# Two attention heads side by side in TensorE's array

## The chip, the cores and the metric

The kernel runs on one core of a Trainium2 chip. The metric is the device time of one execution in microseconds, the median of several runs. One execution was also traced by the hardware profiler; times inside the trace count from the start of its span.

## The reference, cut to what matters

Three transformer-like blocks work on 256 tokens with 1024 features in float32. Three parts of them are attention over heads of width 64, and one is a table lookup with the same shape of product:

```python
# block 1: causal attention, 16 heads (256 tokens are one block of keys)
s = einsum('bhqd,bhjd->bhqj', q, k); p = softmax(where(causal, s, -1e30)); o = einsum('bhqj,bhjd->bhqd', p, v)
# stick-breaking, 8 heads
z = einsum("bhtd,bhsd->bhts", q, k) * scale
a = where(before, exp(log_sigmoid(z) + after), 0.0); o = einsum("bhts,bhsd->bhtd", a, v)
# NSA, 8 heads in 2 groups: compressed, selected and window branches, weighted by gates
o = g[0] * o_c + g[1] * o_s + g[2] * o_w
# PEER routing: 8 heads, two halves of the query against two tables of 128 keys of width 64
```

## The kernel before, in words

Nearly all the work is products of 256 tokens with weights that are streamed from memory in blocks of 128 x 1024. `Stream` loads a block on SP's queue and splits it into two parts, `hi` on ScalarE (L247) and `lo` on VectorE (L248), and each product is three matmuls (`mm3`, L330 to L332; L395 to L397 where tokens lie on the partitions). A block is 24 such matmuls. These are called *ordinary* below.

The attention parts are generators. Each `yield` says what a step costs, and `pump` (L310) runs steps after each block of ordinary matmuls until the block's credit is used up. The framework then arranges the emitted instructions once more, by its own estimate of times, before the program is fixed; each engine runs its own list in that order and waits by semaphores.

A head has 64 features, so its score product uses only 64 of the 128 rows of TensorE's array, and its value product only 64 of the 128 columns. `tile_position` says which half. Two heads lie on the two halves of the partitions. A float32 matmul leaves two records in the trace.

- Block 1's attention, `moba`: `heads()` runs head by head: `scores(h)` (L673) with the softmax behind it on VectorE and ScalarE (`softmax_neg`, L744 to L751), and the three `transposes` (L680) of the head three before. `pv(u)` (L690, L692) makes the values of four heads.
- `stick_breaking`: `part1` (scores, L945 and L946), `part2` (sums by triangular matrices, L961 and L962), `part3` (values, L973 and L974), each two heads behind the one before.
- `nsa`: 16 units (head, branch): `scores` (L1080, L1081), `transposes` (L1087), `pv` (L1099, L1100, and for the second branch the compressed one, L1103). Its bias table `alibi` (L1072) is loaded on POOL's queue, and the pools of its tiles `sm_t`, `ptn` and `alibi` have two buffers each. It takes turns with the HGRN part.
- `routing`: 32 products per half of the tokens (L1408), first all of one row half `a`, then all of the other.

Of the kernel before, what the change touches and what calls it, by code (L numbers as in the profile page):

```python
# [21 lines left out]
P = 128  # L22
T = 256
# [82 lines left out]
def _vectors(inp):  # L106
    """Vectors over features, each as columns of 128."""
# [26 lines left out]
def _constants():  # L134
    """Tables that depend on the shapes alone, side by side in one array of 128 rows."""
# [72 lines left out]
# ---------------------------------------------------------------- the kernel  # L208
class Stream:
    """The weights, block by block: loaded ahead, each split exactly into two float32r parts."""  # L210

    def __init__(self, nc, w, names, raw, hl, ahead=2):
# [4 lines left out]
        # a second pool of two, for the blocks before the given one  # L217
# [10 lines left out]
    def _parts(self, b):  # L228
        # the first block in parts, so that the products start sooner
# [30 lines left out]
class K:  # L260
# [10 lines left out]
    # -- small helpers  # L271
# [23 lines left out]
    # Work that follows the products: `queue` in order, then `fill` (generators that yield what a step costs),  # L295
    # a little after each block of weights, so that the engines that feed the products are never blocked long.
# [30 lines left out]
    # -- products  # L327
# [6 lines left out]
    def lin(self, name, nm, nk, xh, xl, kpb=1, hooks=None, need=None, credit=1.45):  # L334
        """nm column tiles of 128, all of them for each row tile; out [features, tokens]."""
# [13 lines left out]
        # the last two blocks bank by bank, so that the first banks are done sooner  # L349
# [20 lines left out]
    def lin_tok(self, name, xh, xl, w=512, nch=2, hooks=None, credit=1.45):  # L370
        """tokens on partitions: acc[tt][ch] = [128 tokens, 512 features]"""
# [10 lines left out]
        # the last two blocks bank by bank  # L382
# [69 lines left out]
    def root(self, r, ss, width):  # L452
# [8 lines left out]
        # one Newton step: r *= 1.5 - 0.5 * (mean + eps) * r * r  # L461
# [5 lines left out]
    def spread(self, out, r):  # L467
        """The columns of r, by tokens, over the partitions: ones times a diagonal matrix."""
# [11 lines left out]
    # -- parts  # L480
# [139 lines left out]
    def moba(self, need):  # L620
# [3 lines left out]
        with ExitStack() as c:  # L624
# [5 lines left out]
            # two heads (each its first and its second half) on the partitions, pairs of heads in turn  # L630
# [925 lines left out]
```

## Time and profile before

| | |
|---|---|
| median of 3 runs | 1768.69 us (1767.66 to 1768.77) |
| span of the traced execution | 1763.3 us; no time beside the span is recorded for it |
| busy | TensorE 1747.2, VectorE 1311.7, ScalarE 895.1, POOL 27.5 us |
| mean granted TensorE clock | 0.999 |

PE is TensorE's matmuls, PEld its weight loads, DVE is VectorE, ACT ScalarE, SP the queue of the weight loads. In a row of a timeline, "x4" means that four consecutive records of the same line stand together; the second number is the time that they cover, the ends of matmuls being modelled.

### The profile page before, as it was taken

How to read it: one execution, taken by the hardware profiler on the slowest of the kernel's cores; microseconds unless marked ns; L12 is line 12 of the kernel's file. 1: busy time of each engine (PE TensorE's matmuls, PEld its weight loads, DVE VectorE, ACT ScalarE, POOL GpSimd, SP SyncE). 2: the span in 40 equal slices, each digit the busy share in tenths (PEclk: the TensorE clock that was granted, in tenths of full speed). 3: DMA queues.
4: the chain of work that ended last, by engine and by line, in shares of the span. 5: the costliest groups of instructions: out<-in, count | busy, mean ns of one | idle time of the engine just before them, and what ended most of it. 6: DMA issues, size and time to landing. Idle time of an engine off the chain costs nothing.

```text
span 1763.3 us, 33139 instructions
## 1 busy us (share of the span) xinstructions
PE 1747.2 (99%) x13299; PEld 1632.6 (93%) x13299; DVE 1311.7 (74%) x2532; ACT 895.1 (51%) x1324; POOL 27.5 (2%) x66
## 2 busy tenths in 40 slices
PE   8999999999999999999999999999999999999998
PEld 8999999879999998998799999999999888888886
DVE  7779966857997676766588989867776888855555
ACT  6466645556665647535456554533334443345443
POOL 0000000000000000100000000000000000000001
PEclk9999999999999999999999999999999999999999
DMA  7555565545556554632255464644445554455553
GB/s 243 186 180 182 181 200 189 176 135 169 182 178 199 183 176 138 209 114 84 63 192 192 156 206 152 205 133 156 152 148 167 165 171 155 156 179 191 191 191 119
DMA packets 87226, 297.25 MB, mean 169 GB/s; under 512 B 10784, under 2 KB 15680, under 8 KB 87072
## 3 DMA queue, kind: packets, MB, share of 16 engines
q1 hardware_dynamic: 84000, 288.92, 50.4%
q0 software_dynamic: 2640, 5.66, 1.3%
q8 instruction: 104, 1.70, 0.4%
q10 hardware_dynamic: 432, 0.56, 0.1%
q14 instruction: 50, 0.41, 0.1%
HBM read 292.03 MB, written 1.05 MB: 166 GB/s over the span
## 4 chain that ended last, share of the span: by engine, by line
PE 98%; ACT 1%; DVE 0%; issue 0%; DMA 0%; DVEq 0%
PE bank L330 22%; PE bank L331 21%; PE bank L332 21%; PE bank L1318 20%; PE bank L1529 4%; PE bank L396 1%; PE bank L395 1%; PE bank L397 1%; PE bank L673 1%; PE bank L1198 1%; PE bank L1099 1%; PE bank L1081 0%; PE bank L1408 0%; PE bank L1087 0%; PE bank L680 0%; PE bank L1080 0%
## 5 line engine op out<-in xcount | busy, mean ns | idle before, releaser
L247 ACT ACTIVATE hi<-raw 128x1024 fp32r<-128x1024 f32 (+2 forms) x552 | 574.0, 1046 | 731.3 <-PE bank L331 414.8
L248 DVE TENSOR_TENSOR lo<-raw,hi 128x1024 fp32r<-128x1024 f32 (+2 forms) x552 | 662.3, 1206 | 320.4 <-ACT hi L247 317.8
L330 PE MATMUL bank<-xh,hi 128*128 128x256 f32 x2624 | 748.2, 285 | 4.5 <-ACT hi L247 4.5
L331 PE MATMUL bank<-xl,hi 128*128 128x256 f32 x2624 | 743.6, 284 | 0.0
L332 PE MATMUL bank<-xh,lo 128*128 128x256 f32 x2624 | 742.4, 283 | 0.0
L330 PEld LDWEIGHTS bank<-xh,hi 128*128 128x128 f32 x2624 | 503.2, 192 | 9.0 <-ACT hi L247 4.7
L331 PEld LDWEIGHTS bank<-xl,hi 128*128 128x128 f32 x2624 | 503.0, 192 | 1.4 <-issue 1.2
L332 PEld LDWEIGHTS bank<-xh,lo 128*128 128x128 f32 x2624 | 502.7, 192 | 1.1 <-issue 1.1
L1318 PE MATMUL bank<-hi,xh 128*128 128x512 f32 x512 | 161.7, 395 | 0.0
L1318 PE MATMUL bank<-lo,xh 128*128 128x512 f32 x512 | 159.0, 390 | 0.0
L1318 PE MATMUL bank<-hi,xl 128*128 128x512 f32 x512 | 158.9, 390 | 0.0
L1318 PEld LDWEIGHTS bank<-lo,xh 128*128 128x128 f32 x512 | 96.1, 188 | 20.7 <-DVE lo L248 0.3
L1318 PEld LDWEIGHTS bank<-hi,xl 128*128 128x128 f32 x512 | 96.1, 188 | 20.1
L1318 PEld LDWEIGHTS bank<-hi,xh 128*128 128x128 f32 x512 | 94.2, 189 | 17.6
L332 PE MATMUL bank<-ah,lo 128*128 128x256 f32 x352 | 98.9, 281 | 0.0
L330 PE MATMUL bank<-ah,hi 128*128 128x256 f32 x352 | 98.6, 280 | 0.0
L331 PE MATMUL bank<-al,hi 128*128 128x256 f32 x352 | 97.9, 278 | 0.0
L1532 DVE SCALAR_TENSOR_TENSOR H<-bank,H 128x512 f32<-128x512 f32 x64 | 44.0, 687 | 43.4 <-PE bank L1529 43.4
L1529 PE MATMUL bank<-gi,oj 128*128 128x64 f16 x1024 | 74.3, 241 | 0.0
L1529 PEld LDWEIGHTS <-oj 128*128 128x128 f16 x1024 | 62.8, 118 | 9.8 <-issue 4.2
L330 PEld LDWEIGHTS bank<-ah,hi 128*128 128x128 f32 x352 | 66.2, 188 | 0.0
L331 PEld LDWEIGHTS bank<-al,hi 128*128 128x128 f32 x352 | 66.2, 188 | 0.0
(397 smaller groups left out, 1879.4 us busy)
## 6 DMA issues: line engine op xcount, KB each, us to landing
raw<-in_w_dram SPq DMA_DIRECT2D x540, 512.0 KB, 3.4
x<-in_x_dram SPq DMA_DIRECT2D x8, 128.0 KB, 4.1
raw<-in_w_dram SPq DMA_DIRECT2D x8, 128.0 KB, 4.2
alibi<-in_con_dram POOLq DMA_DIRECT2D x8, 128.0 KB, 2.4
raw<-in_w_dram SPq DMA_DIRECT2D x4, 256.0 KB, 4.1
q<-t SPq DMA_DIRECT2D x32, 32.0 KB, 3.2
k<-t SPq DMA_DIRECT2D x32, 32.0 KB, 1.9
wc<-in_wc_dram POOLq DMA_DIRECT2D x2, 512.0 KB, 5.7
```

The costliest lines, as they stand in the source:

```text
L247: nc.scalar.activation(hi[:, c], raw[:, c], AF.Copy)
L248: nc.vector.tensor_tensor(lo[:, c], raw[:, c], hi[:, c].bitcast(F32), ALU.subtract)
L330: mm(out, wh, xh, start=start, stop=False, skip_group_check=True)
L331: mm(out, wh, xl, start=False, stop=False, skip_group_check=True)
L332: mm(out, wl, xh, start=False, stop=stop, skip_group_check=True)
L395: mm(o, xh(k)[:, ts], hi[:, c], start=k == 0, stop=False, skip_group_check=True)
L396: mm(o, xl(k)[:, ts], hi[:, c], start=False, stop=False, skip_group_check=True)
L397: mm(o, xh(k)[:, ts], lo[:, c], start=False, stop=k == NK - 1, skip_group_check=True)
L673: nc.tensor.matmul(o, qa[:, qs], ka[:, 0:ke], start=qs.start == 0, stop=True, skip_group_check=True, tile_position=(rs.start, 0))
L1318: nc.tensor.matmul(acc[tt][n], x[:, s, tt * P:(tt + 1) * P], w[u][:, n * 512:(n + 1) * 512], start=i == 0 and x is self.xh and u == 0, sto ...
L1529: nc.tensor.matmul(b[:, t], oj[:, t // 4, :, t % 4], gi[:, n, t // 4, :, t % 4], start=t + n == 0, stop=n == 1, skip_group_check=True)
L1532: nc.vector.scalar_tensor_tensor(H[:, :, pt], pb.rearrange("p t i -> p i t"), 1.0 / GSCALE, H[:, :, pt], ALU.mult, ALU.mult)
```

## The change: pairs of heads

Two heads that lie on different halves go through all steps together. Their score matmuls alternate between the row halves and fill a bank each; their value matmuls alternate between the column halves. `scores(u)` now takes a pair and returns two banks, the softmax is called by the loop, and the loops of the generators are written anew, with more steps of smaller cost. In block 1 the transposes follow one pair behind instead of three heads. The diff, cut to its core (the values in `stick_breaking` and `nsa` are changed in the way of `moba`'s, and its scores in the way of `moba`'s):

```diff
-            def scores(h):
-                b = self.bank()
-                rs = slice(64 * (h % 2), 64 * (h % 2) + 64)
-                qa, ka = q[rs, h // 2], k[rs, h // 2]
-                for o, qs, ke in ((b[:, 0:128], slice(0, 128), 128), (b[:, 128:384], slice(128, 256), 256)):
-                    nc.tensor.matmul(o, qa[:, qs], ka[:, 0:ke], start=qs.start == 0, stop=True, skip_group_check=True,
-                                     tile_position=(rs.start, 0))
-                return self.softmax_neg(p2, b, causal[:, 128:], causal)
+            def scores(u):
+                bs = [self.bank() for _ in range(2)]
+                for o, qs, ke in ((slice(0, 128), slice(0, 128), 128), (slice(128, 384), slice(128, 256), 256)):
+                    for i in range(2):
+                        rs = slice(64 * i, 64 * i + 64)
+                        nc.tensor.matmul(bs[i][:, o], q[rs, u, qs], k[rs, u, 0:ke], start=qs.start == 0, stop=True,
+                                         skip_group_check=True, tile_position=(64 * i, 0))
+                return bs
...
             def pv(u):
                 b = self.bank()
-                for h in range(4 * u, 4 * u + 4):
-                    o = 256 * (h // 2 % 2)
-                    oo = b[64 * (h % 2):64 * (h % 2) + 64, o:o + 256]
-                    hs = slice(64 * h, 64 * h + 64)
-                    nc.tensor.matmul(oo, v[:, 0, hs], pt[:, h, 0:256], start=h % 4 < 2, stop=False, skip_group_check=True,
-                                     tile_position=(0, 64 * (h % 2)))
-                    nc.tensor.matmul(oo[:, 128:], v[:, 1, hs], pt[:, h, 256:384], start=False, stop=True, skip_group_check=True,
-                                     tile_position=(0, 64 * (h % 2)))
+                for h0 in (4 * u, 4 * u + 2):
+                    o = 256 * (h0 // 2 % 2)
+                    for kt in range(2):
+                        for i in range(2):
+                            h = h0 + i
+                            oo = b[64 * i:64 * i + 64, o + 128 * kt:o + 256]
+                            nc.tensor.matmul(oo, v[:, kt, 64 * h:64 * h + 64], pt[:, h, 0:256] if kt == 0 else pt[:, h, 256:384],
+                                             start=kt == 0 and h % 4 < 2, stop=kt == 1, skip_group_check=True, tile_position=(0, 64 * i))
...
-                for h in range(H + 3):
+                for h in range(0, H + 2, 2):
                     if h < H:
                         self.need(("rope", h // 8))
-                        pr[h] = scores(h)
-                    if h >= 3:
-                        transposes(h - 3, pr.pop(h - 3))
-                    yield 0.7
-                    while "v" in st and 4 * n + 3 <= h - 3:
+                        bs = scores(h // 2)
+                    for i in range(2):
+                        if h >= 2:
+                            transposes(h - 2 + i, pr.pop(h - 2 + i))
+                        if h < H:
+                            pr[h + i] = self.softmax_neg(p2, bs[i], causal[:, 128:], causal)
+                        yield 0.7
+                    while "v" in st and 4 * n + 3 < h:
...
-            for h in range(12):
-                if h < 8:
-                    s1[h] = part1(h)
-                if 0 <= h - 2 < 8:
-                    s2[h - 2] = part2(h - 2, *s1.pop(h - 2))
-                if 0 <= h - 4 < 8:
-                    part3(h - 4, s2.pop(h - 4))
-                yield 0.9
+            for u in range(6):
+                if u >= 2:
+                    part3(u - 2, s2.pop(u - 2))
+                if 0 <= u - 1 < 4:
+                    s2[u - 1] = []
+                    for s in s1.pop(u - 1):
+                        s2[u - 1].append(part2(*s))
+                        yield 0.5
+                if u < 4:
+                    s1[u] = []
+                    for z in part0(u):
+                        s1[u].append(part1(z))
+                        yield 0.4
...
-            s1, s2, al = {}, {}, {0: load_bias(0)}
+            s1, s2, al = {}, {}, {h: load_bias(h) for h in (0, 4)}
             for n in range(len(units) + 2):
-                if n < len(units):
-                    h, br = units[n]
-                    if br == 0:
-                        if n + 2 < len(units):
-                            al[units[n + 2][0]] = load_bias(units[n + 2][0])
-                    s1[n] = scores(h, br, al[h])
-                if 0 <= n - 1 < len(units):
-                    s2[n - 1] = transposes(s1.pop(n - 1))
                 if n >= 2:
                     pv(*units[n - 2], s2.pop(n - 2))
-                yield 0.7
+                if 0 <= n - 1 < len(units):
+                    s2[n - 1] = []
+                    for pr in s1.pop(n - 1):
+                        s2[n - 1].append(transposes(pr))
+                        yield 0.3
+                if n < len(units):
+                    i, br = units[n]
+                    s1[n] = []
+                    for g, b in enumerate(scores(i, br)):
+                        s1[n].append(soften(4 * g + i, br, b))
+                        if br == 1 and i < 3:
+                            al[4 * g + i + 1] = load_bias(4 * g + i + 1)
+                        yield 0.4
...
-                for a in range(2):
-                    for h4 in range(2):
-                        b = self.bank()
-                        for h in range(4):
-                            mm(b[:, h * P:(h + 1) * P], qT[64 * a:64 * a + 64, 4 * h4 + h, tt * P:(tt + 1) * P], sk[64 * a:64 * a + 64],
+                for h4 in range(2):
+                    bs = [self.bank() for _ in range(2)]
+                    for h in range(4):
+                        for a in range(2):
+                            mm(bs[a][:, h * P:(h + 1) * P], qT[64 * a:64 * a + 64, 4 * h4 + h, tt * P:(tt + 1) * P], sk[64 * a:64 * a + 64],
                                start=h == 0, stop=True, skip_group_check=True, tile_position=(64 * a, 0))
```

On TensorE's list, in the middle of block 1's attention, the rows before are two heads, each followed by the transposes of an earlier head:

```order
L673 MATMUL bank<-k,q 128x128
L673 MATMUL bank<-k,q 128x256
L680 MATMUL bank<-c_ident,sm_t 128x128 x3
L673 MATMUL bank<-k,q 128x128
L673 MATMUL bank<-k,q 128x256
L680 MATMUL bank<-c_ident,sm_t 128x128 x3
```

At the same place the rows after are both heads' scores (two matmuls of each shape) and then both transposes:

```order
L674 MATMUL bank<-k,q 128x128 x2
L674 MATMUL bank<-k,q 128x256 x2
L681 MATMUL bank<-c_ident,sm_t 128x128 x6
```

So two visits of scores have become one there.

In the last third of NSA, again on TensorE's list, the rows before show a head's scores (`ns_q`) cut by the transposes (`sm_t`) of the one before:

```order
L1087 MATMUL bank_10407<-c_ident_95,sm_t_10371 128x128
L1080 MATMUL bank_10415<-ns_k_8711,ns_q_8710 128x128
L1087 MATMUL bank_10407<-c_ident_95,sm_t_10371 128x128 x2
L1081 MATMUL bank_10415<-ns_k_8711,ns_q_8710 128x256
L330 MATMUL bank_9935<-xh_103,hi_10237 128x256
```

After the change a place of this kind holds a pair's scores, also cut, then six ordinary matmuls, the values of the pair before (`ptn`) and two more ordinary ones, and then the first transpose of the pair whose scores stand here (`sm_t_10325`):

```order
L1106 MATMUL bank_10313<-c_ident_95,sm_t_10289 128x128
L1096 MATMUL bank_10319<-ns_k_8711,ns_q_8710 128x128
L1106 MATMUL bank_10313<-c_ident_95,sm_t_10289 128x128 x2
L1096 MATMUL bank_10320<-ns_k_8711,ns_q_8710 128x128
L1096 MATMUL bank_10319<-ns_k_8711,ns_q_8710 128x256
L1096 MATMUL bank_10320<-ns_k_8711,ns_q_8710 128x256
...
L1118 MATMUL bank_10381<-ptn_10317,ns_v_8714 64x128
L330 MATMUL bank_9939<-xh_103,hi_10238 128x256
L331 MATMUL bank_9939<-xl_104,hi_10238 128x256
L1106 MATMUL bank_10386<-c_ident_95,sm_t_10325 128x128
```

The first score piece stands alone between two transposes, away from its partner. On ScalarE's list the order after has two ACT_TABLE_LOAD instructions fewer (L458 and L745, in NSA's stretch); the rest of every list holds the same instructions in the same number.

## Rows read from the trace of the kernel before

**Rows 1.** The page: span, and busy time of each engine.
```profile
span 1763.3 us, 33139 instructions
PE 1747.2 (99%) x13299; PEld 1632.6 (93%) x13299; DVE 1311.7 (74%) x2532; ACT 895.1 (51%) x1324; POOL 27.5 (2%) x66
```

**Rows 2.** Busy time of each engine in stretches: us, PE, PEld, DVE, ACT, POOL.
```profile
841.00:880.00 39.00, 38.97 (x223) 26.45 (x222) 22.94 (x84) 18.43 (x53) 3.75 (x7) 1.00 0.22 58
327.00:380.00 53.00, 52.77 (x300) 40.45 (x298) 39.89 (x139) 36.56 (x96) 3.16 (x13) 1.00 0.53 167
970.00:1150.00 180.00, 180.00 (x1520) 179.49 (x1519) 159.85 (x529) 88.95 (x106) 0.00 (x0) 1.00 0.55 179
```

**Rows 3.** Timeline of PE: start, length, line, count. One head's scores; two heads'.
```profile
327.14 0.28 PE L332 MATMUL bank<-xh,lo 128*128 128x256 f32 x1
327.35 0.92 PE L673 MATMUL bank<-k,q 64*128 64x128 f32 x4
...
328.42 0.28 PE L331 MATMUL bank<-xl,hi 128*128 128x256 f32 x1
...
331.26 0.93 PE L673 MATMUL bank<-k,q 64*128 64x128 f32 x8
...
332.35 0.28 PE L331 MATMUL bank<-xl,hi 128*128 128x256 f32 x1
```

**Rows 4.** Timeline of PE: a head's scores followed by transposes.
```profile
342.03 0.92 PE L673 MATMUL bank<-k,q 64*128 64x128 f32 x4
342.88 0.55 PE L680 MATMUL bank<-c_ident,sm_t 128*128 128x128 f32 x3
```

**Rows 5.** Timeline of PE: values of four pairs of heads; of one head alone.
```profile
389.31 0.66 PE L690 MATMUL bank<-pt,v 128*64 128x256 f32 x4
389.79 0.39 PE L692 MATMUL bank<-pt,v 128*64 128x128 f32 x4
...
392.33 0.28 PE L331 MATMUL bank<-ol,hi 128*128 128x256 f32 x1
...
707.79 0.65 PE L973 MATMUL bank<-sb_a,sb_v 128*64 128x256 f32 x2
...
708.81 0.28 PE L331 MATMUL bank<-xl,hi 128*128 128x256 f32 x1
```

**Rows 6.** Timeline of PE: the compressed branch's product of one head, and what follows.
```profile
866.61 0.64 PE L1103 MATMUL bank<-pcT,vc 32*64 32x256 f32 x2
867.18 0.39 PE L332 MATMUL bank<-xh,lo 128*128 128x256 f32 x1
```

**Rows 7.** Timeline of PE: the routing's products for half of the tokens.
```profile
970.28 3.50 PE L1408 MATMUL bank<-sk,qT 64*128 64x128 f32 x32
```

**Rows 8.** Timeline of PE: scores cut by transposes in NSA.
```profile
853.22 0.28 PE L330 MATMUL bank<-xh,hi 128*128 128x256 f32 x1
...
854.32 0.70 PE L1081 MATMUL bank<-ns_k,ns_q 64*128 64x256 f32 x2
...
855.17 0.28 PE L332 MATMUL bank<-xh,lo 128*128 128x256 f32 x1
```

**Rows 9.** Timeline of DVE: the end of that head's softmax.
```profile
856.87 0.55 DVE L751 TENSOR_SCALAR sm_t<-sm_t,sm_r 128x128 f32<-128x128 f32 x2
```

**Rows 10.** Timeline of ACT in the same softmax, and a copy for values.
```profile
855.45 0.40 ACT L745 ACTIVATE sm_t<-sm_t,sm_s 128x128 f32<-128x128 f32 x1 [0.53 <-DVE sm_s L744]
...
856.25 0.18 ACT L745 ACTIVATION_READ_ACCUMULATOR sm_t<-sm_t,sm_s 128x1 f32 x1
856.66 0.49 ACT L1089 ACTIVATE ptn<-bank 128x384 f32<-128x384 f32 x1 [0.23 <-PE bank L1087]
```

**Rows 11.** Timeline of PE: a wait of NSA's values.
```profile
830.08 0.65 PE L1099 MATMUL bank<-ptn,ns_v 128*64 128x256 f32 x2 [0.89 <-ACT ptn L1089]
```

**Rows 12.** Timeline of ACT just before that.
```profile
827.86 1.28 ACT L745 ACT_TABLE_LOAD   x1
```

**Rows 13.** DMA issues of the page: loads of the bias table (KB, us to landing).
```profile
alibi<-in_con_dram POOLq DMA_DIRECT2D x8, 128.0 KB, 2.4
```

More of the change, by code (lines that the diff above doesn't have):

```diff
@@ L939, in stick_breaking, with part0, part1 @@
             mm = nc.tensor.matmul
-            def part1(h):
-                rs = slice(64 * (h % 2), 64 * (h % 2) + 64)
-                qa, ka = q[rs, h // 2], k[rs, h // 2]
-                z = self.bank()
-                mm(z[:, 0:256], ka[:, 0:128], qa, start=True, stop=False, skip_group_check=True, tile_position=(rs.start, 0))
-                mm(z[:, 256:384], ka[:, 128:256], qa[:, 128:256], start=False, stop=False, skip_group_check=True, tile_position=(rs.start, 0))
+            def part0(u):
+                zs = [self.bank() for _ in range(2)]
+                for o, ks, qs in ((slice(0, 256), slice(0, 128), slice(0, 256)), (slice(256, 384), slice(128, 256), slice(128, 256))):
+                    for i in range(2):
+                        rs = slice(64 * i, 64 * i + 64)
+                        mm(zs[i][:, o], k[rs, u, ks], q[rs, u, qs], start=o.start == 0, stop=False, skip_group_check=True,
+                           tile_position=(64 * i, 0))
+                return zs
+            def part1(z):
                 e = p2.tile([P, 384], F32, name="sb_e")
@@ L957, in part1, with part2 @@
                 return z, hi, lo
-            def part2(h, z, hi, lo):
+            def part2(z, hi, lo):
                 for n, s in enumerate((hi, lo)):
@@ L1065, in nsa @@
             yield 3.0
-            units = [(h, br) for i in range(4) for h in (i, 4 + i) for br in range(2)]
+            units = [(i, br) for i in range(4) for br in range(2)]
             def load_bias(h):
@@ L1073, in load_bias, with scores, soften @@
                 return t
-            def scores(h, br, al):
-                g = h // 4
-                gs = slice(64 * g, 64 * g + 64)
-                qa, ka = q[gs, h % 4], k[gs, br]
-                b = self.bank()
-                mm(b[:, 0:128], qa[:, 0:128], ka[:, 0:128], start=True, stop=True, skip_group_check=True, tile_position=(64 * g, 0))
-                mm(b[:, 128:384], qa[:, 128:256], ka, start=False, stop=True, skip_group_check=True, tile_position=(64 * g, 0))
-                return self.softmax_neg(p2, b, al[:, 128:], al, gate=gate[:, :, 3 * h + 1 + br])
+            def scores(i, br):
+                bs = [self.bank() for _ in range(2)]
+                for o, qs, ke in ((slice(0, 128), slice(0, 128), 128), (slice(128, 384), slice(128, 256), 256)):
+                    for g in range(2):
+                        gs = slice(64 * g, 64 * g + 64)
+                        mm(bs[g][:, o], q[gs, i, qs], k[gs, br, 0:ke], start=qs.start == 0, stop=True, skip_group_check=True,
+                           tile_position=(64 * g, 0))
+                return bs
+            def soften(h, br, b):
+                return self.softmax_neg(p2, b, al[h][:, 128:], al[h], gate=gate[:, :, 3 * h + 1 + br])
             def transposes(pr):
@@ L1090, in transposes, with pv @@
                 return pt
-            def pv(h, br, pt):
-                g, i = h // 4, h % 4
-                gs = slice(64 * g, 64 * g + 64)
-                if br == 0 and g == 0 and i % 2 == 0:
+            def pv(i, br, pts):
+                if br == 0 and i % 2 == 0:
                     self.ns_o = self.bank()
-                o = self.ns_o[gs, (i % 2) * T:(i % 2 + 1) * T]
-                vs = slice(128 * br + 64 * g, 128 * br + 64 * g + 64)
-                mm(o, v[:, 0, vs], pt[:, 0:256], start=br == 0 and i % 2 == 0, stop=False, skip_group_check=True, tile_position=(0, 64 * g))
-                mm(o[:, 128:], v[:, 1, vs], pt[:, 256:384], start=False, stop=False, skip_group_check=True, tile_position=(0, 64 * g))
+                oo = [self.ns_o[64 * g:64 * g + 64, (i % 2) * T:(i % 2 + 1) * T] for g in range(2)]
+                for kt in range(2):
+                    for g in range(2):
+                        vs = slice(128 * br + 64 * g, 128 * br + 64 * g + 64)
+                        mm(oo[g][:, 128 * kt:], v[:, kt, vs], pts[g][:, 0:256] if kt == 0 else pts[g][:, 256:384],
+                           start=kt == 0 and br == 0 and i % 2 == 0, stop=False, skip_group_check=True, tile_position=(0, 64 * g))
@@ L1101, in pv @@
                 if br == 1:
                     cs = slice(32 * i, 32 * i + 32)
-                    mm(o, vc[cs, gs], pcT[cs, g], start=False, stop=True, skip_group_check=True, tile_position=(32 * i, 64 * g))
-                    if g == 1 and i % 2 == 1:
+                    for g in range(2):
+                        mm(oo[g], vc[cs, 64 * g:64 * g + 64], pcT[cs, g], start=False, stop=True, skip_group_check=True,
+                           tile_position=(32 * i, 64 * g))
+                    if i % 2 == 1:
```

24 lines of the change are left out of this document (13 added, 11 removed).

## Prediction

> **What bounds the kernel now.** I read the page first. TensorE is busy for 1747.2 of 1763.3 us [rows 1], and the chain of work that ended last is nearly all its own. So time moves only where TensorE's own work changes, or where it is made to wait. The trace has one execution of 1763.3 us, and no time of its own outside that span is recorded for it. The median of the three timed runs, 1768.69, is 5.4 us above it; I add that 5.4 back at the end.
>
> Then I read the four stretches that the diff touches [rows 2]: block 1's attention (327 to 395 us), stick-breaking (672 to 713), NSA (797 to 880) and the routing of PEER (970 to 1150). Shown are the tightest pieces: TensorE is full in each; VectorE has 159.85 of 180 us in the routing, and in the first 53 us of block 1's attention VectorE has 39.89 and ScalarE 36.56. Neither is full.
>
> Last I read what one *visit* costs, that is, a break of the ordinary weight products for a head's products. An ordinary product starts 0.12 us after the one before (a block of 24 takes 2.9 us); the first record of a visit starts 0.21 after (327.14 to 327.35). I take the time from a visit's first record to the second ordinary start behind it, plus that 0.21, less two pitches: minus 0.03.
>
> - Scores of one head alone (4 records): 328.42 - 327.35 - 0.03 = 1.04 us. Scores of heads 1 and 2, which happen to stand next to each other on different row halves (8 records): 332.35 - 331.26 - 0.03 = 1.06 us [rows 3]. **The second head is nearly free.** This pair of rows carries the forecast.
> - Scores inside a chain with transposes: 0.85 us to the next transpose (342.03 to 342.88) and, I take it, 0.1 for the switch back to the whole array, as at the entry (0.21 for 0.12), so 0.95 us a head [rows 4].
> - Values: one head 708.81 - 707.79 - 0.03 = 0.99 us; four pairs of heads in block 1's attention 392.33 - 389.31 - 0.03 = 2.99 us, 0.75 a pair [rows 5]. The column halves already run side by side there.
> - The compressed branch's product adds 867.18 - 866.61 = 0.57 us a head [rows 6].
> - Routing, 32 records of one half after the other: 3.50 us, 0.109 each [rows 7].
>
> **The change, part by part.** The order shows the same matmuls in the same number, and two ScalarE table loads fewer. Nothing is added; heads are brought side by side.
>
> *Scores.* Block 1's attention: 16 heads are 15 visits now (heads 1 and 2 share one) and 8 afterwards: 7 x 0.95 = 6.7 us. Stick-breaking: two pairs of heads already stand together (4 + 4 records in one visit), so 6 visits become 4: 1.9 us. NSA: 16 become 8: 7.6 us. Together 16.2 us.
>
> *Values.* In block 1's attention the four pairs show 0.75 us a pair already, so I take nothing: the program has the 256-wide and the 128-wide product of one head and then those of the next, but the records start as four wide ones and then four narrow ones [rows 5]. The Trainium skill, "TensorE: Matmul & The Clock Gate", Part 3, says that matmuls start and end strictly in program order; by that rule head after head could not overlap, and alternating would gain here too (rival 4 has the price). The order of the starts does not agree with it. In stick-breaking 8 visits become 4 and in NSA 16 become 8. Of 0.99 alone about 0.1 is entry that a chain shares, so 12 x 0.9 = 10.8 us. The compressed products go from 8 to 4: 4 x 0.57 = 2.3 us.
>
> *Routing.* Twice 3.50 us becomes about half (16 x 0.109 = 1.75) plus an entry of 0.2, 1.5 us saved each: 3.0 us. VectorE is busiest there, but TensorE never idles, so I count it.
>
> The gross gain is 16.2 + 10.8 + 2.3 + 3.0 = 32.3 us.
>
> *Cut visits.* The new order sometimes puts a piece of a score or value visit between the transposes of another head (the NSA piece in the section on the change). A cut has a price in the trace: transposes and scores, interleaved, take 855.17 - 853.22 - 0.24 = 1.71 us [rows 8], against 1.04 + 0.36 uncut, so 0.31. Cutting a pair also strands the first piece without a partner (two records, 0.2), so 0.5. I count ten cuts in the new order and five in the old: 10 x 0.5 - 5 x 0.31 = 3.4 us lost.
>
> *Waits.* This is the unknown. Transposes now follow their softmax by one pair where block 1 had three heads between. The softmax of a head takes, from the end of its scores (854.32 + 0.70) to its first third (856.87 + 0.28), 2.13 us with VectorE free [rows 8, 9]. In block 1 a whole block of weights (24 products, 2.9 us) plus the next scores and two transposes stand between, about 4.5 us, which covers both heads. In NSA's last pairs there are six ordinary products, the values of the pair before and two more: 0.82 + 1.0 + 0.24 = 2.06 us for the first head, and some 1.0 more for the second. The second head's exponentials stand behind the first's on ScalarE (0.98 us, from 855.45 to 856.43), and copies of 0.49 get in between [rows 10]. So the wait is near zero for the first head and zero to 1.5 for the second. From below: no wait at all. From above: all 20 pairs wait for both heads' whole chain, 2.13 + 0.98 = 3.1 us, 62 us in all. The row for the real distance, 2.06 against 2.13, lies close to the lower end. I take 0.5 us at six pairs, 3 us. Who stands behind such a wait: all later weight products, so it goes straight to the end.
>
> *Table loads.* Before, 0.89 us of TensorE idling at 830 us sits behind a table load (1.28 us) ahead of a softmax's exponentials [rows 11, 12]. ScalarE's order after the change has that load no more; I take the 0.9 us back.
>
> *Loads of the bias table.* They are issued after the same head's last use and take 2.4 us from issue to landing [rows 13]. The next use is a pair later (about 4.8 us even in the dense end: a pair's steps are charged 1.4 of the 2.3 that a block of 24 products grants, so 1.7 us of those, and 3.1 of its own visits), so I cost it at nothing; if a pair came in under 2.4 us, VectorE would wait for the rest, three times.
>
> Sum: 32.3 - 3.4 - 3.0 + 0.9 = 26.8 us. Span 1763.3 - 26.8 = 1736.5; with the 5.4 outside it, **1741.9 us**.
>
> **Rivals.**
> 1. *The transposes wait, moderately.* If every one of the 20 pairs loses 0.7 us, 14 us of 29.8 (32.3 - 3.4 + 0.9) are eaten: 1768.7 - 29.8 + 14 = 1752.9. For it: in NSA both softmax tiles are double-buffered only, so a pair takes both buffers, and ScalarE gets 2 x 0.98 us of exponentials and two copies in about 4.8 us. Against it: the emitted order puts work between scores and transposes, and the stretch 841 to 880 has VectorE at 22.94 of 39 us [rows 2].
> 2. *The transposes wait, badly: slower.* At more than 29.8 / 20 = 1.5 us a pair the change loses. If the second head always waits for the first's exponentials and both copies, 0.98 + 2 x 0.49 = 1.96 us a pair, that is 39 us: 1778. The place to see it is the transposes of the NSA tail. Against it: block 1's pairs have 4.5 us of cover. The Trainium skill's "TensorEngine Tiling (Array Packing)", section "PSUM Bottleneck", points the same way: packing speeds up TensorE and not what empties PSUM; no row here shows that yet.
> 3. *The halves don't run side by side when they alternate.* Then the change does not do what it says: only entries and exits are saved, 29 visits x 0.2 = 5.8 us, less 3.4 of cuts and 3 of waits, plus 0.9: 1768.4, no change. Against it stand the rows of heads 1 and 2 and of the four pairs.
> 4. *Block 1's values gain as well.* If the two heads of a pair overlap only in part today, alternating helps there too: at most a head's stream without entry, 0.99 - 0.34 = 0.65 us, for each of eight pairs, 5.2 us more, 1736.7. The four pairs at 0.75 us each speak against it, since one head alone takes 0.99 with its entry. (By the rule of the Trainium skill quoted under the values it would be so.)
>
> **How the numbers follow.** The forecast (1735 to 1748) gets 0.74, the moderate waits 0.12, the bad waits 0.04, no overlap 0.04, the fourth 0.06. Within 0.2% (3.5 us, about what a measurement of this kernel can tell from no change) lies mainly the third. So faster 0.92, same 0.04, slower 0.04. The range reaches from rival 4 without the 3 us of waits (1733.7, so 1734) to just past the moderate waits, 1754.
>
> **What the new profile would show.** Right: score visits of 8 records taking about 0.95 us, value visits of a pair in NSA about 1 us, a routing visit near 1.9 us, NSA's stretch about 16 us shorter, block 1's attention about 6, stick-breaking about 5. Wrong: idle time of TensorE before the transposes ending on VectorE's scaling of sm_t (rivals 1 and 2), or 8 records taking near 1.8 us (rival 3).

## The result, and the profile after

The changed kernel takes 1740.62 us (median of four runs, 1740.35 to 1740.91) against 1768.18 us of the kernel before beside it: the ratio is 0.9847, with a 95% interval of 0.9835 to 0.9859. The forecast was 1741.9 us, within 1.3 us.

The profiled execution has a time of 1740.35 us. First its page (span, busy times), which answers [rows 1]:

```profile
span 1738.6 us, 33154 instructions
...
PE 1721.9 (99%) x13299; PEld 1617.3 (93%) x13299; DVE 1310.0 (75%) x2532; ACT 889.7 (51%) x1322; POOL 27.6 (2%) x66
```

The span is 24.7 us shorter and TensorE's busy time 25.3 us, with the same 13299 matmul records. So what went is time on TensorE itself, not waiting. The stretches that answer [rows 2] (us, then PE, PEld, DVE, ACT, POOL, granted clock):

```profile
327.00:391.00 64.00, 61.91 (x425) 49.91 (x424) 45.52 (x146) 40.80 (x103) 3.18 (x13) 1.00 0.54 170
788.00:857.50 69.50, 68.82 (x517) 55.97 (x517) 52.37 (x192) 39.08 (x104) 6.33 (x12) 1.00 0.31 92
948.00:1115.00 167.00, 167.00 (x1432) 166.33 (x1432) 151.84 (x516) 84.81 (x101) 0.00 (x0) 1.00 0.55 180
```

VectorE has come nearer to full (52.37 of 69.5 us in NSA, 151.84 of 167 in the routing), but TensorE still fills each stretch.

Where the time came from is read by taking the same ordinary matmul (the first, the hundredth and so on) in both traces and comparing its start. The lead of the changed kernel is -0.2 us ahead of block 1's attention (the small difference is from the start of the program) and 4.4 behind it, 4.3 ahead of stick-breaking and 9.5 behind it, 22.4 behind NSA, 22.1 ahead of the routing and 24.9 behind its two halves, and 24.7 from there on. So block 1 gave 4.6 us, stick-breaking 5.2, the stretch with NSA 12.9 and the routing 2.8; between them, three pieces of 0.2 to 0.3 us went the other way. A piece of 0.3 at one of these places also lies between two executions of the changed kernel itself, so they need not come from the change.

The visits themselves, in the timeline of TensorE: a pair's scores alone, a pair's scores followed by six transposes, a pair's values alone, and one half of the routing, the first three with products behind them. They answer [rows 3], [rows 4], [rows 5] and [rows 7].

```profile
327.57 0.93 PE L674 MATMUL bank<-k,q 64*128 64x128 f32 x8
...
328.65 0.28 PE L331 MATMUL bank<-xl,hi 128*128 128x256 f32 x1
...
341.00 0.93 PE L674 MATMUL bank<-k,q 64*128 64x128 f32 x8
341.86 0.87 PE L681 MATMUL bank<-c_ident,sm_t 128*128 128x128 f32 x6
342.49 0.47 PE L395 MATMUL bank<-hi,xh 128*128 128x512 f32 x1
...
684.37 0.87 PE L984 MATMUL bank<-sb_a,sb_v 128*64 128x256 f32 x8
...
685.39 0.28 PE L331 MATMUL bank<-xl,hi 128*128 128x256 f32 x1
...
948.16 2.06 PE L1433 MATMUL bank<-sk,qT 64*128 64x128 f32 x32
```

Two heads' scores, 8 records, now cost 328.65 - 327.57 - 0.03 = 1.05 us (one head: 1.04 before). Two heads' values cost 685.39 - 684.37 - 0.03 = 0.99 us, the price of one head before. The routing's 32 records cover 2.06 us, not 3.50.

Not all pairs stayed whole. In the same view, a pair of block 1's is taken apart into its two heads, and a pair of NSA's scores (L1096) is cut by the spreads of the gates (L477):

```profile
363.24 0.89 PE L674 MATMUL bank<-k,q 64*128 64x128 f32 x4 [0.30 <-DMA k<-t]
364.06 0.50 PE L397 MATMUL bank<-lo,xh 128*128 128x512 f32 x1
...
364.73 0.92 PE L674 MATMUL bank<-k,q 64*128 64x128 f32 x4
...
817.65 0.92 PE L1096 MATMUL bank<-ns_k,ns_q 64*128 64x128 f32 x4
818.50 0.71 PE L477 MATMUL bank<-rs_d,ones 128*128 128x128 f32 x4
819.14 0.49 PE L1096 MATMUL bank<-ns_k,ns_q 64*128 64x128 f32 x2
819.55 0.49 PE L477 MATMUL bank<-rs_d,ones 128*128 128x128 f32 x2
819.97 0.70 PE L1096 MATMUL bank<-ns_k,ns_q 64*128 64x256 f32 x2
820.60 0.39 PE L330 MATMUL bank<-xh,hi 128*128 128x256 f32 x1
```

In both, the four records of one head cover about what eight cover in a whole pair (0.89 to 0.92, and 0.93), so the second head has lost its free ride. Four other pairs of NSA's scores are cut by transposes in such a way that only their first piece stands alone. Here is an uncut chain of transposes, scores and values, and then a cut one up to its values, which start at 844.32:

```profile
831.83 0.49 PE L1106 MATMUL bank<-c_ident,sm_t 128*128 128x128 f32 x3
832.25 0.93 PE L1096 MATMUL bank<-ns_k,ns_q 64*128 64x128 f32 x8
833.10 1.16 PE L1118 MATMUL bank<-ptn,ns_v 128*64 128x256 f32 x8
...
842.47 0.27 PE L1106 MATMUL bank<-c_ident,sm_t 128*128 128x128 f32 x1
842.67 0.48 PE L1096 MATMUL bank<-ns_k,ns_q 64*128 64x128 f32 x2
843.09 0.44 PE L1106 MATMUL bank<-c_ident,sm_t 128*128 128x128 f32 x2
843.46 0.93 PE L1096 MATMUL bank<-ns_k,ns_q 64*128 64x256 f32 x6
```

And what TensorE waits for, its idle time before a matmul by what ended it (total us, times, longest):

```profile
PE bank L330 <- ACT oh L400: 1.6, 1, 1.6
...
PE bank L681 <- DVE sm_t L755: 0.2, 1, 0.2
```

The first is block 1's output product. The waits on a softmax, which the prediction feared, are one of 0.2 us, and the 0.89 us of [rows 11] are gone. A wait inside a pair does not show as idle time, though: at 833.10 above, the second head's values start 0.29 us behind the first's, right after ScalarE's copy of that head's transposed weights (`ptn`) ends at 833.34, and the visit covers 1.16 us, where others cover 0.87.

### The profile page after: what moved, and what is told of

It reads as the page before. It is cut to its first block, busy times and chain, and to the rows that moved or that the text cites. A ratio compares the mean times of both kernels' runs of the same rounds, so it can differ in the third digit from the quotient of the medians.

```text
span 1738.6 us, 33154 instructions
## 1 busy us (share of the span) xinstructions
PE 1721.9 (99%) x13299; PEld 1617.3 (93%) x13299; DVE 1310.0 (75%) x2532; ACT 889.7 (51%) x1322; POOL 27.6 (2%) x66
## 3 DMA queue, kind: packets, MB, share of 16 engines
HBM read 292.03 MB, written 1.05 MB: 169 GB/s over the span
## 4 chain that ended last, share of the span: by engine, by line
PE 95%; DVE 1%; DMA 1%; ACT 1%; SPq 1%; issue 0%; DVEq 0%; ACTq 0%
PE bank L330 21%; PE bank L332 21%; PE bank L331 21%; PE bank L1343 20%; PE bank L1555 4%; PE bank L397 1%; PE bank L396 1%; PE bank L395 1%; PE bank L1223 1%; DMA raw<-in_w_dram 1%; SPq L666 1%; PE bank L1096 0%; PE bank L1118 0%; PE bank L1106 0%; ACT hi L247 0%
```

## The experiments

Each is an edit of the changed kernel; spans are compared with its 1738.6 us, and a stage's change is read by the starts of the same ordinary matmuls.

**Is it the alternation, or only that the two heads stand side by side?** Within a pair, one head's two matmuls and then the other's:

```diff
-                for o, qs, ke in (...):
-                    for i in range(2):
+                for i in range(2):
+                    for o, qs, ke in (...):
```

> Pairs as in the change, but inside a pair's scores and values the program has one head's two matmuls and then the other's (block 1, stick-breaking, NSA; the routing still alternates). Theory: what pays is that the two heads stand in one visit; TensorE starts the other half's work past the same half's next matmul, as the four wide and four narrow value records before the change showed. Then a pair's score visit stays at 8 records of 0.93 us and an NSA value visit near 1.16 us, and the time within 2 us of the changed kernel's 1740.6. Rival: the alternation in the program is what pays. Then the 20 score pairs go to about 1.8 us (0.85 more each) and the 12 value pairs of stick-breaking and NSA lose up to 0.65: 17 + 8 = 25 us, about 1765.

Measured: 1740.93 us, ratio to before 0.9845 (0.9829 to 0.9862). TensorE's list of this kernel has head after head in the whole pairs, and the trace's single records show it: in nearly all of them the second head's records start 13 to 14 ns behind the first's, as at heads 1 and 2 of the kernel before (13), where those of the changed kernel start 6 to 7 ns behind. The visit is as long as with alternation, and the rival's 25 us do not appear:

```profile
327.78 0.93 PE L674 MATMUL bank<-k,q 64*128 64x128 f32 x8
```

The next run was made because this list was taken for an alternating one; its expectation says so, and is wrong there. In it, each matmul is held behind the one before it:

```diff
+                        with (tc.issue_after(ins) if ins is not None else ExitStack()):
+                            ins = nc.tensor.matmul(...).ins
```

> Head after head again, this time held: each matmul of a pair's scores and values (block 1's scores, stick-breaking, NSA) must be issued after the one before it, so that TensorE's own order has one head's two matmuls and then the other's. In the first run of this kind the scheduler had put nearly all pairs back into alternation, so it told nothing about the order. Theory (adjacency pays; TensorE starts the other half's matmul past the same half's next one, as the heads 1 and 2 of the kernel before, 1.06 us for two, and the runs of two in the routing, 2.16 against 2.06 us, let it): a pair's 8 score records stay at 0.93 us and a value pair at 0.88, time 1740 to 1742. Rival (alternation pays): 8 records take 1.57 us as on one row half, 20 score pairs at 0.65 and 12 value pairs at 0.5 to 0.65 make 19 to 21 us, about 1760.

Here, too, TensorE's list has head after head in the score pairs and in the value pairs of stick-breaking and NSA; block 1's values alternate as in the changed kernel. Measured: 1741.49 us (1741.38 to 1742.97), ratio 0.9859 (0.9843 to 0.9876). The same visit as above, in this kernel:

```profile
328.25 0.93 PE L676 MATMUL bank<-k,q 64*128 64x128 f32 x8
...
329.34 0.28 PE L331 MATMUL bank<-xl,hi 128*128 128x256 f32 x1
```

Still 0.93 us for two heads, and 1.06 with its entry and exit. The rival's 1.57 (below) does not appear. In both runs the four 128-wide records of such a visit start before the four 256-wide ones, so the second head's first matmul starts ahead of the first head's second. Alternation in the list is not needed; that the heads stand side by side is (the runs with scores and values apart, below). The span is 1739.6 us, and stick-breaking alone is 1.35 us longer, where the list came out arranged otherwise (1.36 in the first run); block 1 is 0.4 us shorter in both. The Trainium skill, "TensorE: Matmul & The Clock Gate", Part 3, holds that matmuls start strictly in program order; by that, these eight records could not lie in 0.93 us. The measurement decides against it here.

**Is it the two halves of the rows, or fewer visits?** In block 1 the pairs are formed of heads h and h + 2, which lie on the same row half; the order of the heads changes with it.

```diff
-                    for i in range(2):
-                        rs = slice(64 * i, 64 * i + 64)
+                    for i, h in enumerate(pair):
+                        rs = slice(64 * (h % 2), 64 * (h % 2) + 64)
```

> Block 1 alone: the two heads of a pair are taken from the same half of the rows (h and h + 2), so that the visits stay 8 and the order stays the same but nothing in a score pair can run side by side. Theory (overlap of the halves pays, predicted 0.95 us a head for scores): a pair's 8 score records go from 0.93 to 1.6 to 1.8 us, and block 1's attention grows by 8 x 0.65 to 8 x 0.85 = 5.2 to 6.8 us. Rival (rival 3 of the prediction: only entries and exits are saved): 8 records stay near 0.93 us and block 1's attention within 1 us.

```profile
327.49 1.57 PE L674 MATMUL bank<-k,q 64*128 64x128 f32 x8
```

Measured: 1744.02 us (one run), span 1742.2. A whole pair takes 1.57 us, not 0.93: 0.64 us a pair is what the halves give by running side by side. Block 1 grew by 3.9 us, less than expected, because two of the eight pairs are cut in this arrangement (one in the changed kernel); six whole ones at 0.64 make 3.8. Rival 3 falls.

**How far past its own half does TensorE reach?** In the routing, runs of two matmuls of one half and then two of the other for the first half of the tokens, runs of four for the second.

```diff
-                    for h in range(4):
-                        for a in range(2):
+                    n = (2, 4)[tt]
+                    for h0 in range(0, 4, n):
+                        for a, h in ((a, h) for a in range(2) for h in range(h0, h0 + n)):
```

> Routing alone: instead of strict alternation, runs of two matmuls of one half, then two of the other (first half of the tokens), and runs of four (second half). Before the change runs of eight took 3.50 us for 32 records, alternation takes 2.06. Theory (TensorE takes a matmul of the other half past at least one of its own half): runs of two stay at 2.06 to 2.3 us; runs of four lie between, about 2.4 to 3.0. Rival (only neighbours in the program overlap): in runs of two one boundary in two overlaps, so half of the gain is lost, about 2.8 us; with runs of four 3.1 to 3.2.

```profile
948.25 2.16 PE L1434 MATMUL bank<-sk,qT 64*128 64x128 f32 x32
...
1033.62 2.82 PE L1434 MATMUL bank<-sk,qT 64*128 64x128 f32 x32
```

Measured: 1741.00 us (one run), span 1739.2. Here the list was as written. Runs of one take 2.06 us, of two 2.16, of four 2.82, of eight 3.50 [rows 7]. Two in a row cost next to nothing, and four lose half of what alternation gains over eight. Runs of eight are not without overlap either: in the single records of the kernel before, three starts follow another record's by 4 to 6 ns, all where the two halves meet in the list. Runs of four have three such places with three such starts each, so a meeting is worth about (3.50 - 2.82) / 2 = 0.34 us. An attention pair, two matmuls a head, therefore needs no alternation, while the routing does.

**What are the terms worth?** Scores written head by head, each with its softmax, values still in pairs:

```diff
-                        bs = scores(h // 2)
                     for i in range(2):
+                        if h < H:
+                            bs = scores(h // 2, i)
```

> Scores of a pair written head by head, each followed by its softmax, in all three attentions; values stay in pairs. In the order of TensorE most pairs of block 1 are apart by it (transposes or ordinary products between), and most of NSA's come together again. Theory (the score term: 0.95 us a head in block 1, of which 0.65 is the overlap and the rest entry and switches): each pair of block 1 that is apart costs 0.85 to 0.95 more, six or seven of them 5.1 to 6.7 us; stick-breaking 1 to 2 us; 1746 to 1750. Rival (rival 3: only entries and exits): 0.2 to 0.3 a pair, 1742 to 1743.

Measured: 1749.29 us (one run), span 1747.5. Block 1 grew by 4.8 us and stick-breaking by 2.6; in NSA (0.9) five of the eight pairs came together again in TensorE's list. Another 1.2 us lie ahead of block 1, where the edit changes nothing. A pair of block 1 that is apart:

```profile
360.09 0.92 PE L674 MATMUL bank<-k,q 64*128 64x128 f32 x4
360.94 0.55 PE L681 MATMUL bank<-c_ident,sm_t 128*128 128x128 f32 x3
361.42 0.92 PE L674 MATMUL bank<-k,q 64*128 64x128 f32 x4
362.27 0.55 PE L681 MATMUL bank<-c_ident,sm_t 128*128 128x128 f32 x3
362.57 0.48 PE L395 MATMUL bank<-hi,xh 128*128 128x512 f32 x1
```

Scores and transposes take 362.57 - 360.09 = 2.48 us from the first score to the next ordinary matmul, and 342.49 - 341.00 = 1.49 with the pair whole: 0.99 us, where the prediction had 0.95. Of that 0.64 is the overlap (above), and 0.35 is going back and forth between the half array and the whole.

Values written apart, with a part of the next pair's work between; scores still in pairs:

```diff
-                    pv(*units[n - 2], s2.pop(n - 2))
+                    pv(*units[n - 2], s2[n - 2], 0)
...
+                        if i == 1 and n >= 2:
+                            pv(*units[n - 2], s2[n - 2], 1)
                         s2[n - 1].append(transposes(pr))
```

> Stick-breaking and NSA: the values (and the compressed products) of the two heads of a pair are written apart, with a part of the next pair's work between; scores stay in pairs. Some of them come together again in the order of TensorE, so the price is read per pair that is apart. Theory (the value term, 0.9 us a visit removed, 0.57 a compressed product): a pair that is apart costs 0.65 to 0.9 us more, and about six are apart: 4 to 6 us, with the compressed products up to 7; 1744 to 1748. Rival (values of two heads overlap no better in a pair than apart; the gain in NSA came from the scores): under 1.5 us.

Measured: 1748.10 us (one run), span 1746.3. Stick-breaking grew by 1.9 us with three pairs apart (one of them also stood apart in the changed kernel), NSA by 6.2 with six (two of them also parted in the changed kernel). In NSA, a pair with its compressed products (L1127), apart in this kernel and then whole in the changed one:

```profile
850.16 0.86 PE L1122 MATMUL bank<-ptn,ns_v 128*64 128x256 f32 x4
850.96 0.64 PE L1127 MATMUL bank<-pcT,vc 32*64 32x256 f32 x2
851.53 0.86 PE L1122 MATMUL bank<-ptn,ns_v 128*64 128x256 f32 x4
852.32 0.64 PE L1127 MATMUL bank<-pcT,vc 32*64 32x256 f32 x2
852.89 0.39 PE L331 MATMUL bank<-xl,hi 128*128 128x256 f32 x1
```

```profile
844.32 0.87 PE L1118 MATMUL bank<-ptn,ns_v 128*64 128x256 f32 x8
845.12 0.65 PE L1123 MATMUL bank<-pcT,vc 32*64 32x256 f32 x4
845.70 0.39 PE L331 MATMUL bank<-xl,hi 128*128 128x256 f32 x1
```

852.89 - 850.16 = 2.73 against 845.70 - 844.32 = 1.38: 1.35 us a pair. The second head's values are 852.32 - 851.53 = 0.79 of it and its compressed product 852.89 - 852.32 = 0.57. The prediction had 0.9 + 0.57 = 1.47. With nine pairs apart and not six, the whole loss is more than the 4 to 7 us expected. The gain of the values is real and nearly as large as costed.

**What would it cost if pairs were never cut?** The four matmuls of a pair's scores or values bound together, so that nothing stands between them:

```diff
+                with tc.tile_critical():
                     for o, qs, ke in (...):
```

> The four matmuls of a pair's scores or values are bound together so that nothing is scheduled between them (all three attentions, but not block 1's values); the written-down order also crowds more pairs into fewer visits. Theory: what the change still loses is cut visits; the trace shows one score visit in NSA cut by the gates' spread at about 1.6 us, a value visit cut at about 1.0, and four or five smaller cuts. With no cuts the time falls by 3 to 5 us, to about 1736. Rival (waits: rivals 1 and 2 of the prediction): the crowded visits leave too little ordinary work between a pair's scores and its transposes, TensorE idles there 1 to 2 us a pair, and the time is the same or up to 10 us later.

Measured: 1846.95 us, ratio 1.0458 (1.0429 to 1.0488). The theory's edit failed at its purpose: bound pairs also moved together into a few dense visits and each of them waits for other work first, so it does not price the cuts alone. But it shows what the bad rivals look like. Idle time of TensorE by releaser, its stretches (the number behind the POOL busy time is the granted clock), and a score visit:

```profile
PE bank L675 <- DMA raw<-in_w_dram: 14.4, 4, 5.3
PE bank L682 <- DVE sm_t L756: 8.7, 5, 3.0
```

```profile
300.00:330.00 30.00, 30.00 (x253) 30.00 (x252) 22.22 (x38) 12.50 (x14) 0.00 (x0) 1.00 0.57 193
...
345.00:360.00 15.00, 7.18 (x34) 4.17 (x34) 6.88 (x35) 6.30 (x22) 0.00 (x0) 0.50 0.11 37
360.00:385.00 25.00, 24.75 (x108) 19.90 (x104) 12.11 (x26) 12.30 (x21) 0.00 (x0) 0.93 0.38 105
```

```profile
341.25 1.65 PE L675 MATMUL bank<-k,q 64*128 64x128 f32 x8 [5.30 <-DMA raw<-in_w_dram]
```

Transposes wait for the softmax just as rivals 1 and 2 had it, up to 3.0 us each. The largest single item, however, is one that no rival named: TensorE waits 14.4 us for weight blocks ahead of block 1's scores. And the waits come with a lower clock: up to 330 us TensorE was busy throughout at a granted clock of 1.00; from 345 to 360 us it was busy 7.18 of 15 us at 0.50 (1.2 GHz, the lower of its two levels), and the same 8 records, behind 5.30 us of idling, took 1.65 us, not 0.93. Block 1 alone lost 42 us.

**Why did block 1 give 4.6 us and not more?** The pair that was taken apart (heads 12 and 13) costs 1.40 us, 0.30 of it waiting for k, and 1.05 for its second head, where a whole one costs 0.95. The moves that bring q's and k's heads into place (L666) take SyncE 5.5 us for eight. They were split over two queues:

```diff
-                        nc.sync.dma_start(dst[o:o + 32, 2 * a + r // 2], ...)
+                        (nc.sync if x == 0 else nc.gpsimd).dma_start(dst[o:o + 32, 2 * a + r // 2], ...)
```

> Block 1 alone: the moves that set q's and k's heads apart go half over SyncE's queue and half over GpSimd's, instead of all over SyncE's, where eight issues take 5.5 us in a row. Theory: block 1 gave 1.6 us less than predicted because the pair of heads 12 and 13 waits 0.30 us for k and is taken apart (1.40 + 1.05 us for its two halves against 0.95 for a pair together); with k there earlier the pair stays together, block 1's attention is 1.2 to 1.5 us shorter, the time 1739.2 to 1739.5. Rival: what takes the pair apart is not the transfer but the order in which the program puts the two heads (they stand apart there too, with ordinary products between); then only the 0.30 us of waiting goes, or nothing.

```profile
363.46 1.30 PE L674 MATMUL bank<-k,q 64*128 64x128 f32 x8
```

The pair is together again (though the second head still starts later, 1.30 for 0.93) and block 1 is 0.9 us shorter (1.2 to 1.5 were expected). Yet the time is 1741.39 us (1740.78 to 1741.51): from the last move of the output on SyncE's queue to the end of the span pass 4.8 us and not 3.0. The mechanism is right, and the gain is given back at the close of the program. The next try put only four moves on ScalarE's queue:

```diff
+                        (nc.scalar if x and a == 3 and dst is k else nc.sync).dma_start(...)
```

> The changed kernel, with only the last four moves that bring k's heads 12 to 15 into place issued by ScalarE instead of SyncE. Theory: as with the two queues before, the pair of heads 12 and 13 stays together (8 score records in one visit of about 1.6 us with the first transposes, for 1.40 + 1.05 before), block 1 is 0.8 to 1.2 us shorter, and GpSimd's part of the program's close is not lengthened by 1.7 us this time, so the gain shows: 1739.4 to 1739.8. Rival: four issues on ScalarE (0.5 to 0.6 us each) delay the exponentials and copies of the pair before, and TensorE waits 0.5 us or more for its transposes: no change, 1740.3 to 1741.

```profile
364.05 2.43 SPq L666 DMA_DIRECT2D k<-t  x4
```

```profile
365.92 1.53 PE L674 MATMUL bank<-k,q 64*128 64x128 f32 x8 [2.47 <-DMA k<-t]
```

Measured: 1743.86 us (1742.65 to 1744.88). Neither theory: the four moves that stayed with SyncE were issued later (364.05 us, where the eight began at 360.19), and TensorE waited 2.47 us for the last of them. Eight moves on GpSimd's queue, half of those of heads 12 to 15:

```diff
+                        (nc.gpsimd if x and a == 3 else nc.sync).dma_start(...)
```

> The changed kernel, with eight of the moves (half of those of q's and k's heads 12 to 15) on GpSimd's queue instead of 32 as in the run with two queues. Theory: the last k arrives as early as there, the pair of heads 12 and 13 stays together, block 1 is 0.8 to 1.5 us shorter; GpSimd's part of the close is lengthened only by about a quarter of what 32 moves cost, which stays behind SyncE's part: span 1737.3 to 1737.9, time 0.7 to 1.4 us under the changed kernel's beside it. Rival: the order of the moves shifts as in the run with ScalarE's queue and the pair waits for k for 1 us or more, or the close is again 1.7 us longer: no gain, or 1 to 2 us later.

> The changed kernel, unchanged, beside the run with eight moves on GpSimd's queue, for a comparison on one chip. Every theory: 1740.3 to 1741.2, span 1738.5 to 1739.3.

Measured: 1740.02 us (1739.36 to 1740.72) with the eight moves, ratio 0.9841 (0.9828 to 0.9855), and 1740.86 (1740.80 to 1743.60) for the changed kernel beside it. Block 1 is 0.9 us shorter, the close is 3.0 us again, and the span is 1738.0 against 1739.0 us. So it is a better version by about 0.8 us, 0.05%: the profile shows where, the times alone would hardly.

**What lies outside the span?** The kernel before, unchanged, with a profile once more:

> The kernel before, unchanged, once more with a profile: its first profiled execution had a span of 1763.3 us, 5.4 under the median of its times, while every run since shows only 1.7 to 1.8 us outside the span. Theory: the median's surplus is not time outside the span but a longer span at a lower granted clock (spans of 1765 to 1769 go with 0.995 to 0.998); a profile of such a run shows a stretch with the clock below 1.00, behind a stretch in which TensorE idled. Rival: time outside the span varies between executions; then the span is again near 1763 and the time 4 to 5 us above it.

```profile
span 1763.5 us, 33139 instructions
```

Its time was 1765.31 us, so 1.8 us lie outside. The rival falls. The other executions of the kernel before list spans of 1766.5 to 1767.3 us at a granted clock of 0.996 to 0.997 in the same set; in another, 1763.2 us went with 0.999 and 1769.5 with 0.995. So most of the median's surplus over the traced execution goes with the clock. The part of the theory that a profile would show the stretch remains open: both traced executions of the kernel before had 0.999.

## Why the prediction was right, and where its steps were off

The medians differ by 27.6 us, the spans of the two traced executions by 24.7. The difference between these goes with the clock of the kernel before in its other executions (mostly 0.996 to 0.998, where the changed one has 0.998 to 0.999); what lowers it there was not found.

- **Side by side is what pays: right.** Scores of a pair cost what one head cost; this rested on heads 1 and 2 [rows 3], which stood head after head in the list. The two runs with head after head show that the reading was sound, the run on one row half that it is the halves.
- **The unit prices: slightly high.** Scores 0.95 a head removed; measured 0.99 where transposes stand between, but in block 1 as a whole (4.8 us for seven visits, with 1.5 us already lost in the changed kernel at the pair taken apart) 0.9. Values 0.9; measured 0.8. Compressed 0.57; measured 0.57. Routing 3.0; measured 2 x (3.50 - 2.06) = 2.9 (its rows before already held one meeting of the halves). With these the gross sum is 17 x 0.9 + 12 x 0.8 + 4 x 0.57 + 2.9 = 30.1 us, not 32.3.
- **Cuts: rightly priced, but the dearest kind was missing.** A pair of NSA's scores cut by the transposes was costed at 0.5 us. From the first transpose to the values a cut pair takes 844.32 - 842.47 = 1.85 us and an uncut one 833.10 - 831.83 = 1.27, so 0.58. But where a cut parts the two heads, the second loses its partner: 1.5 us in block 1 (1.40 + 1.05 - 0.95), and in NSA 820.60 - 817.65 = 2.95 us for one pair's scores and six records of spreads. The term had no such case. By the rows: 1.5 in block 1; in NSA some 1.5 there (2.95 less 0.95 for a whole pair and 0.5 for the spreads, four of which alone take 815.57 - 815.21 = 0.36), four cuts by transposes at 0.58, two value pairs parted at up to 0.8, and one more of these in stick-breaking: 7.7 us and not 5.0.
- **Waits: costed too high.** 3.0 us were taken for the transposes; they wait 0.2. Block 1's output product waits 1.6 us (1.2 before), a product of the HGRN part 0.4 (L1200, none before), block 1's scores 0.3 for k, and 0.3 are lost inside the value pair at 833.10. That the distance of 2.06 us lies so close to the 2.13 of the softmax was true, but the framework had put enough between. That waits cost much where it does not is shown by the run with bound pairs, though not for the softmax alone; rivals 1 and 2 were the right ones to name.
- **Table load: right in size.** The 0.9 us at NSA's values went; no run takes out the load alone, so that it was the cause is argued.
- **Block 1's values, at nothing: right.** The last four pairs take 2.94 us (2.99 before, [rows 5]); rival 4 falls. The first run with head after head says why: it has these values head after head too, as the list before, and their 32 records cover 2.87 us as before, against 2.82 alternated.
- **The 5.4 us outside the span: wrong.** It is 1.7 to 1.8 us in the runs of both kernels (1740.35 - 1738.6; 1765.31 - 1763.5). The rest was a traced execution that ran at a higher clock than the median. The predicted span, 1736.5, was 2.1 us too short; the addition was 3.6 us too long. The two errors hide each other in the forecast of 1741.9, so that it came within 1.3 us is luck in part.

With measured terms the sum is 30.1 gross, less 7.7 of cuts, plus 1.6 for the five cuts that the kernel before had, less 1.0 of waits (0.2, 0.4 more at the output product, 0.4 at L1200) and 0.3 inside the value pair, plus 0.9: 23.6 us against the 24.7 of the spans. The 1.1 between them is not assigned; stick-breaking alone gave 5.2 us, where these terms make 2 x 0.9 + 4 x 0.8 - 0.8 = 4.2. By stages the prediction had about 16 us for NSA, 6 for block 1 and 5 for stick-breaking, and 12.9, 4.6 and 5.2 came: what fell short lies in NSA and block 1, where most of the parted pairs are.

## What to carry to other kernels

Small matmuls that use half of the array's rows or columns should stand beside one on the other half; in runs of two their order did not matter here; longer runs are better alternated. A pair is worth only what keeps it whole: look in the trace for visits with half of the records at the full length, and ask what its second member came late for. Binding it by force can cost far more than the cut, because waits behind a dense visit go straight into TensorE's time.

## What the runs showed of the hardware that was not expected

- TensorE starts a matmul of the other half ahead of the next one of its own half in the list. Runs of two lose almost nothing by it (2.16 us for 2.06); in longer runs only three starts at each place where the halves meet come in pairs (2.82 us with runs of four, 3.50 with runs of eight). The order in the list shows in the trace by how far the second head's records start behind the first's: 6 to 7 ns alternated, 13 to 14 head after head.
- In the one trace with 32 short moves on GpSimd's queue early in the program, the program's close took 4.8 us; with eight, and in every other trace, 3.0. What makes it longer is not shown.
- The granted clock fell to 0.50 in a stretch where TensorE was busy 7.18 of 15 us, and was 0.93 in the next, where it was busy 24.75 of 25.
